# More pauses in two recurrences' instruction streams, UV's copies first, and an output projection by token halves with accumulators that end apart

## The chip, the core and the metric

The kernel runs on one core of one Trainium2 chip. The core has a matrix engine (TensorE, PE in the profile), a vector engine (VectorE, DVE), a scalar engine (ScalarE, ACT), GpSimd (POOL) and a sync engine (SP) that issues most transfers. The metric is the device time of one execution in microseconds, less being better. Three runs of the kernel before took 2685.09, 2686.59 and 2689.0 us, with a median of 2686.59 us.

## The reference

A decoder layer over 2048 tokens of width 1024, in float32. One input projection feeds two groups of heads, HGRN2 (a gated linear recurrence) and RWKV-7 (a recurrence with a vector-valued state update). Their outputs are concatenated, projected by `w_out` and added to `x`; a ConvFFN follows, and a last normalization.

```python
h = _rmsnorm(x, norm1_w[l])
proj = h @ w_in[l]
...
o_hg = _hgrn2_mixer(q_raw, f_raw, i_raw, g_raw, lower_bounds[l], hg_norm_w[l])
...
o_rw = _rwkv7_mixer(r, k, v, wd, ad, gd, ...)
x = x + jnp.concatenate([o_hg, o_rw], axis=-1) @ w_out[l]
x = x + _conv_ffn(_rmsnorm(x, norm2_w[l]), w_up[l], conv_w[l], conv_b[l], w_down[l])
```

## The kernel before

Tokens go through in four blocks of 512 (`nb` from 0 to 3). Phase 1 makes the input projection, both recurrences and the output projections of blocks 0 to 2; phase 2 makes the output projection of block 3 and the ConvFFN. The change touches phase 1 alone.

**Products in three passes.** A float32 product is computed as three matmuls of operands split in a high and a low part (`mm3`, lines 265, 266 and 267): high with high, high with low, low with high. I call these three a triple. A split (line 249 and line 250, or lines 242 and 243 for `split_to`) is a rounding copy on ScalarE and a subtraction on VectorE.

**Three streams.** `phase1` has three Python generators that write out instructions: `dense` (projections, transposes, output blocks), `rw_stream` (eight calls of `rw_super`, two for each token block) and `hg_stream` (16 calls of `hg_unit`, four for each token block). The loop at lines 1077 to 1084 goes in rounds: one step of `rw_stream`, one step of `hg_stream`, and then `fill(TICK)`, which takes steps of `dense` until 2000 ns of credit are used. A triple of a projection counts 648, one of an output block 680, whatever it takes on the chip. A step of a recurrence ends at a `yield`; with a `yield None` a stream says that its input isn't ready. So a `yield` more at one place lets one more portion of dense work stand between two steps of that recurrence. `dense` itself waits on counts of finished recurrence steps (`done`).

The Tile framework derives all dependencies, hands out buffers from a free pool for each tag (`bufs=4` means four buffers), and may issue ready instructions ahead of earlier ones that are not. The functions of ScalarE that need a table (`act`, line 112) keep the program's order among themselves.

**RWKV.** A step of `rw_super` makes a part of one chunked update for two head pairs. At line 702 `KB` is completed; at line 757 the inputs of the next super are released; lines 798 to 809 make `z` and copy it to `ZT`; lines 811 to 823 make `z2`. Lines 825 to 829 are the matmuls whose results are copied first to `M` (three copies, lines 831 to 834) and then to `UV` (four copies, lines 835 to 839). After the following `yield`, lines 844 to 850 multiply `KBT` with `UV`, and lines 851 to 863 use `M`. Lines 879 to 888 go through the eight chunks with the state `XH`.

**HGRN.** In `hg_unit`, lines 1003 to 1005 scale `k` and `q`; after a `yield`, lines 1010 to 1016 transpose `k` and make `KT`; after another, lines 1020 to 1026 use `KT` for the states.

**Output block.** `out_block` (line 373) goes through four passes, token halves `i2` by column halves `dh`. A pass has two accumulators (`accs`, tag `pj`, two PSUM banks that the projections use too), one for each 128 tokens, and eight slices `k` of the contracted dimension. For each slice the weights are loaded by POOL's queue (`woraw`, line 389) and split into `wh` and `wl` (tag `w`, four buffers each, which the projections' weights use as well); two triples follow, one for each accumulator. For blocks 0 and 1 the first pass also loads the recurrences' output `oT` slice by slice for all 512 tokens (line 382, staging tag `sg` with two buffers) and splits it into `hh` and `hl`. For block 2 the first 256 tokens were split before (`oh`, `ol`), and the others are loaded slice by slice in the third pass (line 386). At slice 6 two tiles of `x` are loaded (`xh`); at the end of the pass both accumulators are added to them (line 407) and stored (line 409). In the last pass `next_block` splits the next token block's input into `hh` and `hl`, two slices behind.

Of the kernel before, what the change touches and what calls it, by code (L numbers as in the profile page):

```python
# [7 lines left out]
F32 = mybir.dt.float32  # L8
# [10 lines left out]
P = 128  # L19
# [45 lines left out]
def tile_layer(ctx, tc, consts, x, norm1_w, w_in, hg_lb_logits, hg_norm_w, rw_shift_mu, rw_w0, rw_w2,  # L65
# [46 lines left out]
    def act(out_, in_, func, **kw):  # L112

        want = tables.get(func)
        if want is not None and want != tab["now"]:
            pre = S.preload_act_table_set(want)
# [3 lines left out]
        i_ = S.activation(out_, in_, func, **kw)  # L120
# [120 lines left out]
    def split_to(hi, lo, src):  # L241
        S.copy(hi, src)
        V.tensor_sub(lo, src, hi.bitcast(F32))

    def split(pool, src, shape, name, bufs):

        hi = pool.tile(shape, F32R, tag=name + "h", name=name + "h", bufs=bufs)
        lo = pool.tile(shape, F32R, tag=name + "l", name=name + "l", bufs=bufs)
        S.copy(hi, src)  # L249
        V.tensor_sub(lo, src, hi.bitcast(F32))  # L250
        return hi, lo
# [11 lines left out]
    def mm3(acc, lhs, rhs, first, last, skip=False):  # L263
        (lh, ll), (rh, rl) = lhs, rhs
        TE.matmul(acc, lh, rh, start=first, stop=False, skip_group_check=skip)  # L265
        TE.matmul(acc, lh, rl, start=False, stop=False, skip_group_check=skip)  # L266
        TE.matmul(acc, ll, rh, start=False, stop=last, skip_group_check=skip)  # L267

    def phase1(c1):
# [21 lines left out]
        def bank(kind):  # L291
            return ps.tile([P, 512], F32, tag=kind, name=kind, bufs=2)
# [7 lines left out]
        def stg(tag, name, bufs):  # L300
            return sp.tile([P, BLK], F32, tag=tag, name=name, bufs=bufs)
# [71 lines left out]
        def out_block(nb, oh=None, ol=None, then=None):  # L373


            for i2 in range(2):
                for dh in range(2):
                    accs = [bank("pj") for _ in range(2)]
                    for k in range(KD):
                        if i2 == 0 and dh == 0 and oh is None:  # L380
                            raw = stg("sg", "oraw", 2)
                            dma(raw, oT[nb][k * P:(k + 1) * P, :])
                            split_to(hh[:, k, :], hl[:, k, :], raw)
                        if i2 == 1 and dh == 0 and oh is not None:
                            raw = stg("sg", "oraw", 2)[:, 0:256]
                            dma(raw, oT[nb][k * P:(k + 1) * P, 256:512])
                            split_to(hh[:, k, 256:512], hl[:, k, 256:512], raw)
                        raw = wp.tile([P, 512], F32, tag="wraw", name="woraw", bufs=4)
                        wload(raw, w_out[0, k * P:(k + 1) * P, dh * 512:dh * 512 + 512])
                        wh, wl = split(wp, raw, [P, 512], "w", 4)  # L390
                        if k == KD - 2:
                            inputs = dh == 0 and (i2 == 0) == (oh is None)
                            xh = [wp.tile([P, BLK], F32, tag="wraw", name="xh", bufs=4) if inputs else
                                  stg("sg", "xh", 2) for _ in range(2)]
                            for q in range(2):
                                t0 = nb * BLK + (i2 * 2 + q) * P
                                dma(xh[q], x[0, t0:t0 + P, dh * 512:dh * 512 + 512])
                        for q in range(2):
                            is_ = slice((i2 * 2 + q) * P, (i2 * 2 + q + 1) * P)
                            lhs = ((hh[:, k, is_], hl[:, k, is_]) if oh is None or i2 == 1 else  # L400
                                   (oh[k // 4][:, k % 4, is_], ol[k // 4][:, k % 4, is_]))
                            mm3(accs[q], lhs, (wh, wl), k == 0, k == KD - 1)
                            if i2 == 1 and dh == 1 and q == 1:
                                next_block(then, k)
                            yield 680
                    for q in range(2):
                        V.tensor_add(xh[q], accs[q], xh[q])
                        r0 = (i2 * 2 + q) * P
                        dma(x1d[nb][r0:r0 + P, dh * 512:dh * 512 + 512], xh[q])

        rows = {}

# [225 lines left out]
        def rw_super(nb, s_):  # L638

            tl = stage[("tl", nb)]  # L640
            r, k, v = (stage.pop(("rkv", nb, s_, w)) for w in range(3))
            prs = (2 * s_, 2 * s_ + 1)
            pc = [slice(p * P, (p + 1) * P) for p in prs]

# [3 lines left out]
            def bank2():  # L648
                return ps.tile([P, 2, BLK], F32, tag="rw", name="rw", bufs=2)
# [52 lines left out]
            V.tensor_mul(KB[:, :, 1:3, :], v16(c), v16(a))  # L702
            V.tensor_mul(BV, b1, v)
            yield

            M = tile_("M", [2, 2, 4, 2, P], "M")
            for j in range(2):
# [48 lines left out]
            act(RHS[0:64, :, :, 0:64], tpv[64:128], AF.Copy)  # L756
            done["rw1"] += 1
            yield

            lv = bank2()  # L760
            for b, h, e, u in quads():
# [42 lines left out]
            for u in U:  # L804
                for e in range(2):
# [2 lines left out]
                    act(ZT[r1:r1 + 32, 8 * u:8 * u + 8],  # L808
                        z[c0:c0 + 32, 0, u * 256:u * 256 + 256].rearrange("p (s t) -> p s t", t=32), AF.Copy)
            yield  # L810
            z2 = bank2()
            for b, h, e, u in quads():
                r0 = er0(e)
# [17 lines left out]
            act(M[:, 0, 0, :, :, 0:64], quv[0][:, :, :, 0:64], AF.Copy)  # L831
            for e in range(2):
                r0, c0 = er0(e), col0(1, e)
                act(M[r0:r0 + 64, 0, 1, :, :, 0:64], quv[1][c0:c0 + 64, :, :, 0:64], AF.Copy)
            for u in U:
                for e in range(2):
                    r0, c0 = er0(e), col0(u, e)
                    act(UV[r0:r0 + 64, 4 * u:4 * u + 4, e, :].rearrange("p b (h t) -> p b h t", t=64),
                        quv[u][c0:c0 + 64, :, :, 64:128], AF.Copy)
            yield  # L840
            XH = tile_("XH", [2, 9, 64], "XH")
            V.tensor_copy(XH[:, :, 0, :], Xc[:, 2 * s_:2 * s_ + 2, :])
            xp = bank2()
# [79 lines left out]
        def hg_unit(nb, j):  # L923
# [79 lines left out]
            X = scaled(6)  # L1003
            V.tensor_mul(k, k, Sf)
# [12 lines left out]
            yield  # L1017
# [557 lines left out]
```

## Time and profile before

| | us |
|---|---|
| median of three runs | 2686.59 |
| the profiled execution's own time | 2686.26 |
| its span, from the first to the last instruction | 2684.5 |
| matmuls on PE, busy | 2614.7 |
| VectorE busy | 1929.6 |
| ScalarE busy | 1338.3 |
| PE busy in the first 100 us | 83.6 |
| PE busy from 1100 to 1200 us | 94.4 |
| PE busy from 1300 to 1400 us | 91.3 |

How to read it: a row of instructions has the engine, the line of the kernel, the operation, the tiles as out<-in, and the shapes. PEld are the weight loads, which run beside the matmuls. In a timeline the first two numbers are start and duration in us, and a bracket at the end gives the idle time before the row and what ended it. A row of waits reads "who line <- what it waited for: us in total, times, longest". A window's row gives its length, the busy time of PE, PEld, DVE, ACT and POOL with the number of instructions, the granted clock of PE as a share, the DMA engines' busy share and GB/s. Matmuls are pipelined: the duration shown (0.39 us for 128x512) includes the time in the pipe, and start to start they follow each other faster.

### The profile page before, as it was taken

What the parts mean: (1) busy time and instruction counts of PE and PEld (TensorE: products, weight loads), DVE (VectorE), ACT (ScalarE), POOL (GpSimd) and SP (SyncE); (2) the same over time, 40 slices, a digit from 0 to 9 for tenths busy, and PEclk for the clock granted to TensorE, in tenths of its full rate; (3) what the DMA queues carried; (4) which work ended last, traced back from release to release, by engine and by line L of the source; (5) the groups of instructions that cost most, each with busy time, mean ns of one, the idle gap of its engine ahead of it and who ended that gap; (6) DMA issues with size and microseconds to landing.
All of it is one profiled execution on the core that took longest, in us unless ns stands there. A gap on an engine that the chain in (4) does not pass through costs nothing.

```text
span 2684.5 us, 47831 instructions
## 1 busy us (share of the span) xinstructions
PE 2614.7 (97%) x18059; PEld 2091.1 (78%) x18059; DVE 1929.6 (72%) x3705; ACT 1338.3 (50%) x2158; POOL 381.8 (14%) x684
## 2 busy tenths in 40 slices
PE   7999999999999999999999999999999999999998
PEld 5777777777777777778778888887888888788887
DVE  4867757576466764657578789988998888676556
ACT  4555442454544545433357665456555545445444
POOL 6433222212222123222100000000000000000000
PEclk9999999999999999999899999999999999999999
DMA  8654543355643556834584458756764463898665
GB/s 304 198 166 162 166 135 117 115 161 195 197 149 116 157 161 214 290 115 132 160 272 149 134 184 267 243 171 194 259 200 149 149 202 124 311 325 282 203 192 184
DMA packets 312828, 510.52 MB, mean 190 GB/s; under 512 B 46879, under 2 KB 143509, under 8 KB 312597
## 3 DMA queue, kind: packets, MB, share of 16 engines
q1 hardware_dynamic: 258225, 329.65, 37.2%
q0 software_dynamic: 54304, 177.80, 20.3%
q8 instruction: 142, 2.33, 0.4%
q14 instruction: 89, 0.73, 0.1%
q10 hardware_dynamic: 68, 0.02, 0.0%
HBM read 373.13 MB, written 134.22 MB: 189 GB/s over the span
## 4 chain that ended last, share of the span: by engine, by line
PE 74%; DVE 7%; DMA 6%; issue 6%; ACT 5%; POOL 1%; SPq 0%; DVEq 0%; POOLq 0%; ACTq 0%
PE pj L265 8%; PE pj L266 7%; PE pj L267 7%; PE ua L265 5%; PE ua L267 5%; PE ua L266 5%; PE da L266 3%; PE da L267 3%; PE da L265 3%; PE ud L266 2%; PE ud L265 2%; PE ud L267 2%; PE hg L969 2%; PE db L265 2%; PE db L266 2%
## 5 line engine op out<-in xcount | busy, mean ns | idle before, releaser
L265 PE MATMUL pj<-hh,wh 128*128 128x512 f32 x960 | 404.1, 421 | 4.5 <-ACT rkv L120 1.7
L266 PE MATMUL pj<-hl,wh 128*128 128x512 f32 x960 | 377.9, 394 | 0.0
L267 PE MATMUL pj<-hh,wl 128*128 128x512 f32 x960 | 377.7, 394 | 0.0
L265 PE MATMUL ua<-Bh,uwh 128*128 128x512 f32 x704 | 275.9, 392 | 1.0 <-ACT m L120 0.9
L267 PE MATMUL ua<-Bh,uwl 128*128 128x512 f32 x704 | 274.3, 390 | 0.0
L266 PE MATMUL ua<-Bl,uwh 128*128 128x512 f32 x704 | 274.1, 389 | 0.0
L265 PEld LDWEIGHTS pj<-hh,wh 128*128 128x128 f32 x960 | 181.2, 189 | 59.6 <-issue 14.0
L267 PEld LDWEIGHTS pj<-hh,wl 128*128 128x128 f32 x960 | 181.0, 189 | 40.1 <-issue 0.6
L266 PEld LDWEIGHTS pj<-hl,wh 128*128 128x128 f32 x960 | 181.5, 189 | 38.7 <-issue 5.9
L249 ACT CAST uwh<-uraw 128x512 fp32r<-128x512 f32 x220 | 135.1, 618 | 138.0 <-PE ua L266 63.2
L250 DVE TENSOR_TENSOR dal<-draw,dah 128x512 fp32r<-128x512 f32 x138 | 95.3, 690 | 113.1 <-ACT dah L249 113.0
L250 DVE TENSOR_TENSOR uwl<-uraw,uwh 128x512 fp32r<-128x512 f32 x220 | 147.3, 686 | 34.8 <-ACT uwh L249 34.8
L249 ACT CAST dah<-draw 128x512 fp32r<-128x512 f32 x138 | 85.8, 622 | 167.3 <-PE da L266 78.7
L265 PEld LDWEIGHTS ua<-Bh,uwh 128*128 128x128 f32 x704 | 132.2, 188 | 29.8 <-ACT m L120 2.4
L267 PEld LDWEIGHTS ua<-Bh,uwl 128*128 128x128 f32 x704 | 132.2, 188 | 28.1 <-DVE uwl L250 0.4
L266 PEld LDWEIGHTS ua<-Bl,uwh 128*128 128x128 f32 x704 | 132.2, 188 | 26.6
L265 PE MATMUL ud<-Bh,uwh 128*128 128x512 f32 x352 | 138.0, 392 | 0.0
L267 PE MATMUL ud<-Bh,uwl 128*128 128x512 f32 x352 | 137.0, 389 | 0.0
L266 PE MATMUL ud<-Bl,uwh 128*128 128x512 f32 x352 | 137.0, 389 | 0.0
L1445 POOL DMA_DIRECT2D gd<-y x2 | 1.1, 556 | 947.0 <-DVE y L1443 947.0
L266 PE MATMUL da<-dbl,dah 128*128 128x512 f32 x332 | 129.5, 390 | 1.1 <-DVE dbl L250 1.1
L267 PE MATMUL da<-dbh,dal 128*128 128x512 f32 x332 | 129.2, 389 | 0.0
(570 smaller groups left out, 6199.2 us busy)
## 6 DMA issues: line engine op xcount, KB each, us to landing
uraw<-in_w_up_dram SPq DMA_DIRECT2D x176, 256.0 KB, 3.3
woraw<-in_w_out_dram POOLq DMA_DIRECT2D x96, 256.0 KB, 3.4
br<-gd SPq DMA_DIRECT2D x88, 256.0 KB, 4.1
draw<-Sg SPq DMA_DIRECT2D x88, 256.0 KB, 3.0
draw<-Tw SPq DMA_DIRECT2D x88, 256.0 KB, 3.5
gd<-y SPq DMA_DIRECT2D x86, 256.0 KB, 2.8
Sg<-br SPq DMA_DIRECT2D x72, 256.0 KB, 2.6
xt<-x1d SPq DMA_DIRECT2D x32, 512.0 KB, 5.9
```

Source lines behind the costliest of these rows:

```text
L249: S.copy(hi, src)
L250: V.tensor_sub(lo, src, hi.bitcast(F32))
L265: TE.matmul(acc, lh, rh, start=first, stop=False, skip_group_check=skip)
L266: TE.matmul(acc, lh, rl, start=False, stop=False, skip_group_check=skip)
L267: TE.matmul(acc, ll, rh, start=False, stop=last, skip_group_check=skip)
L969: TE.matmul(o, kt[:, t0:t0 + 64], qs, start=True, stop=True, tile_position=(0, e * 64))
L1445: (dma if end is None else nc.gpsimd.dma_start)(gd_[2 * h + b][fb * P:(fb + 1) * P, :], ys[0][:, b * BLK:(b + 1) * BLK])
```

## The change

Four things. `rw_super` takes an additional `yield` at four places (after lines 704, 758, 810 and 840) for the first six of its eight calls. `hg_unit` takes one more at two places (after lines 1006 and 1017) for the first 14 of its 16 calls. The four copies to `UV` come ahead of the three copies to `M`. And `out_block` is rewritten in two ways: `oT` is loaded and split by token halves, two slices at a time, the first half in pass one and the second in pass two (for block 2 only the second half); and the second accumulator runs one slice behind the first, so that the first one ends two triples earlier, and each is added and stored as soon as it ends. The tiles for `x` come from the weights' staging tag in the first pass of blocks 0 and 1 only, else from `sg`.

```diff
                     accs = [bank("pj") for _ in range(2)]
+                    ws, first_pass = [], oh is None and i2 == 0 and dh == 0
+                    pairs = {0: (0, 1), 2: (2,), 4: (3,)} if first_pass else {m: (m,) for m in range(4)}
                     for k in range(KD):
-                        if i2 == 0 and dh == 0 and oh is None:
-                            raw = stg("sg", "oraw", 2)
-                            dma(raw, oT[nb][k * P:(k + 1) * P, :])
-                            split_to(hh[:, k, :], hl[:, k, :], raw)
-                        if i2 == 1 and dh == 0 and oh is not None:
-                            raw = stg("sg", "oraw", 2)[:, 0:256]
-                            dma(raw, oT[nb][k * P:(k + 1) * P, 256:512])
-                            split_to(hh[:, k, 256:512], hl[:, k, 256:512], raw)
+                        if i2 == 0 and (dh == 1 or oh is None):
+                            hs = slice(256 * dh, 256 * dh + 256)
+                            for m in pairs.get(k, ()):
+                                raw = stg("sg", "oraw", 2).rearrange("p (k t) -> p k t", k=2)
+                                dma(raw, oT[nb][2 * m * P:(2 * m + 2) * P, hs].rearrange("(k p) t -> p k t", p=P))
+                                split_to(hh[:, 2 * m:2 * m + 2, hs], hl[:, 2 * m:2 * m + 2, hs], raw)
...
-                        wh, wl = split(wp, raw, [P, 512], "w", 4)
+                        ws.append(split(wp, raw, [P, 512], "w", 4))
...
-                        for q in range(2):
+                        for q, kq in ((0, k), (1, k - 1), (1, k if k == KD - 1 else -1)):
+                            if kq < 0:
+                                continue
...
-                            mm3(accs[q], lhs, (wh, wl), k == 0, k == KD - 1)
-                            if i2 == 1 and dh == 1 and q == 1:
+                            mm3(accs[q], lhs, ws[kq], kq == 0, kq == KD - 1)
+                            if kq == KD - 1:
+                                V.tensor_add(xh[q], accs[q], xh[q])
+                                r0 = (i2 * 2 + q) * P
+                                dma(x1d[nb][r0:r0 + P, dh * 512:dh * 512 + 512], xh[q])
+                            if i2 == 1 and dh == 1 and q == 1 and (kq == k or k < KD - 1):
                                 next_block(then, k)
                             yield 680
-                    for q in range(2):
-                        V.tensor_add(xh[q], accs[q], xh[q])
-                        r0 = (i2 * 2 + q) * P
-                        dma(x1d[nb][r0:r0 + P, dh * 512:dh * 512 + 512], xh[q])
...
+            more = range(1 if 2 * nb + s_ < 6 else 0)
...
             yield
+            for _ in more:
+                yield
...
+            for u in U:
+                for e in range(2):
+                    r0, c0 = er0(e), col0(u, e)
+                    act(UV[r0:r0 + 64, 4 * u:4 * u + 4, e, :].rearrange("p b (h t) -> p b h t", t=64),
+                        quv[u][c0:c0 + 64, :, :, 64:128], AF.Copy)
             act(M[:, 0, 0, :, :, 0:64], quv[0][:, :, :, 0:64], AF.Copy)
...
-            yield
+            for _ in range(2 if 4 * nb + j < 14 else 1):
+                yield
```

More of the change, by code (lines that the diff above doesn't have):

```diff
@@ L378, in out_block @@
                     accs = [bank("pj") for _ in range(2)]
+                    ws, first_pass = [], oh is None and i2 == 0 and dh == 0
+                    pairs = {0: (0, 1), 2: (2,), 4: (3,)} if first_pass else {m: (m,) for m in range(4)}
                     for k in range(KD):
-                        if i2 == 0 and dh == 0 and oh is None:
-                            raw = stg("sg", "oraw", 2)
-                            dma(raw, oT[nb][k * P:(k + 1) * P, :])
-                            split_to(hh[:, k, :], hl[:, k, :], raw)
-                        if i2 == 1 and dh == 0 and oh is not None:
-                            raw = stg("sg", "oraw", 2)[:, 0:256]
-                            dma(raw, oT[nb][k * P:(k + 1) * P, 256:512])
-                            split_to(hh[:, k, 256:512], hl[:, k, 256:512], raw)
+                        if i2 == 0 and (dh == 1 or oh is None):
[4 more added lines that the diff above has]
+                                split_to(hh[:, 2 * m:2 * m + 2, hs], hl[:, 2 * m:2 * m + 2, hs], raw)
                         raw = wp.tile([P, 512], F32, tag="wraw", name="woraw", bufs=4)
                         wload(raw, w_out[0, k * P:(k + 1) * P, dh * 512:dh * 512 + 512])
-                        wh, wl = split(wp, raw, [P, 512], "w", 4)
+                        ws.append(split(wp, raw, [P, 512], "w", 4))
                         if k == KD - 2:
-                            inputs = dh == 0 and (i2 == 0) == (oh is None)
-                            xh = [wp.tile([P, BLK], F32, tag="wraw", name="xh", bufs=4) if inputs else
+                            xh = [wp.tile([P, BLK], F32, tag="wraw", name="xh", bufs=4) if first_pass else
                                   stg("sg", "xh", 2) for _ in range(2)]
@@ L758, in rw_super @@
             yield
+            for _ in more:
+                yield
             lv = bank2()
@@ L810, in rw_super @@
             yield
+            for _ in more:
+                yield
             z2 = bank2()
@@ L830, in rw_super @@
             quv = [qus[u].rearrange("p j (b h t) -> p (j b) h t", h=2, t=P) for u in U]
[L831 to L834, printed above, removed]
             for u in U:
@@ L839, in rw_super @@
                         quv[u][c0:c0 + 64, :, :, 64:128], AF.Copy)
+            act(M[:, 0, 0, :, :, 0:64], quv[0][:, :, :, 0:64], AF.Copy)
+            for e in range(2):
+                r0, c0 = er0(e), col0(1, e)
+                act(M[r0:r0 + 64, 0, 1, :, :, 0:64], quv[1][c0:c0 + 64, :, :, 0:64], AF.Copy)
             yield
+            for _ in more:
+                yield
             XH = tile_("XH", [2, 9, 64], "XH")
@@ L1016, in hg_unit @@
             act(Af[0:64, :, 64:128], lp[0:64, 0:256].rearrange("p (b t) -> p b t", t=64), AF.Copy)
-            yield
+            for _ in range(2 if 4 * nb + j < 14 else 1):
+                yield
             SH = rp.tile([P, 5, P], F32, tag="SH", name="SH")
```

5 lines of the change are left out of this document (3 added, 2 removed).

## The prediction

> **What bounds the kernel now.** I read the page's busy times first.
>
> ```profile
> span 2684.5 us, 47831 instructions
> ...
> PE 2614.7 (97%) x18059; PEld 2091.1 (78%) x18059; DVE 1929.6 (72%) x3705; ACT 1338.3 (50%) x2158; POOL 381.8 (14%) x684
> ...
> PE 74%; DVE 7%; DMA 6%; issue 6%; ACT 5%; POOL 1%; SPq 0%; DVEq 0%; POOLq 0%; ACTq 0%
> ```
>
> TensorE is the bound, and the change removes none of its matmuls. It can gain only from PE's idle time, 2684.5 - 2614.7 = 69.8 us, and from time in which PE runs slowly. Everything touched lies in phase 1, whose last output block ends near 1350 us. So next the waits of PE in the window from 0 to 1350 us (total, times, longest):
>
> ```profile
> PE rw L848 <- ACT UV L120: 6.5, 6, 2.0
> PE pj L265 <- ACT hh L242: 6.4, 5, 2.2
> ...
> PE pj L265 <- DVE xh L407: 2.6, 4, 1.0
> PE hg L1011 <- DVE hk L1004: 2.4, 1, 2.4
> ...
> PE rw L815 <- ACT ZT L120: 1.5, 3, 0.8
> PE rw L885 <- DVE XH L887: 1.4, 3, 0.6
> ...
> PE pj L266 <- DVE wl L250: 0.9, 3, 0.4
> PE hg L1022 <- ACT KT L120: 0.8, 2, 0.4
> ...
> PE rw L714 <- DVE KB L702: 0.7, 2, 0.5
> PE pj L265 <- ACT wh L249: 0.7, 2, 0.4
> ```
>
> All but the XH row stand at places that the diff edits. None is long: this is a change of 20 us at most in 2686.
>
> The profiled execution took 2686.26 us, of which 2684.5 are the span; the median of the three runs is 2686.59. The sum below starts from 2686.26, and the 0.3 us between them are nothing here.
>
> **Pauses: do they cost rounds?** Each round of phase 1 runs one step of the RWKV stream, one of the HGRN stream, then 2000 ns of credit of dense work, where a triple of matmuls (L265 to L267) costs 648 or 680. I stepped the three generators through their yields and conditions (a count, no time): dense work never finds its condition unmet and sets 386 rounds, with the pauses as without. The streams wait 63 and 143 rounds for their inputs now, and would wait 39 and 115: 24 pauses (6 supers of 4) and 28 (14 units of 2) fit into these waits. A pause is therefore free as long as dense work is what lasts. If that were wrong, each of 24 would cost a round, 3.1 triples.
>
> A triple is three issue intervals of 0.23 us; the timeline of PE around the HGRN stall shows one at full clock, then the stall, then slow intervals:
>
> ```profile
> 1109.45 0.39 PE L266 MATMUL pj<-hl,wh 128*128 128x512 f32 x1
> 1109.67 0.39 PE L267 MATMUL pj<-hh,wl 128*128 128x512 f32 x1
> 1112.46 0.71 PE L1011 MATMUL hg<-ident,hk 128*128 128x128 f32 x4 [2.40 <-DVE hk L1004]
> ...
> 1115.17 0.63 PE L267 MATMUL pj<-hh,wl 128*128 128x512 f32 x1
> 1115.60 0.63 PE L265 MATMUL pj<-hh,wh 128*128 128x512 f32 x1
> ```
>
> So a triple is 0.69 us, and a pause puts 3.1 x 0.69 = 2.1 us of dense work in front of the next step. For UV the copies' order counts too:
>
> ```profile
> 151.21 1.80 ACT L120 ACTIVATE M<-rw 128x512 f32<-128x512 f32 x3
> ...
> 153.03 2.43 ACT L120 ACTIVATE UV<-rw 64x512 f32<-64x512 f32 x4
> ...
> 154.27 2.27 PE L848 MATMUL rw<-UV,KBT 128*64 128x64 f32 x64 [2.02 <-ACT UV L120]
> ```
>
> The three M copies (1.80 us) stand ahead of the UV copies that L848 waits for. With UV first these 1.80 us leave the wait in all eight supers; M is next needed by L862, behind the 2.2 us of L848, which cover it. Copy order and pause together clear all **6.5**. The pauses ahead of KT, behind KB and behind z take 0.8, 0.7 and 1.1 (the last super is not paused, so not all of ZT's 1.5); the 2.4 of L1011 lose 2.1. Sum: **11.2 us**.
>
> **Output projection.** Windows of the first and the third output block:
>
> ```profile
> 569.00:655.00 86.00, 81.76 (x941) 59.27 (x940) 65.92 (x146) 46.11 (x79) 15.20 (x29) 1.00 0.52 159
> ...
> 1295.00:1350.00 55.00, 49.93 (x448) 38.15 (x446) 33.47 (x74) 22.64 (x40) 8.11 (x15) 0.94 0.48 155
> ```
>
> In the third block (PE idle 5.1 of 55 us) the second token half is loaded in the pass that uses it, through two staging buffers:
>
> ```profile
> L386 SPq DMA_DIRECT2D oraw<-oT x8: 319/319/332, 1308.3 to 1324.8; - x8
> ...
> DMA to landing us min/median/max: 2.5/3.2/9.5
> ```
>
> and PE's waits from 1290 to 1350 us give the price:
>
> ```profile
> PE pj L265 <- ACT hh L242: 3.6, 2, 2.2
> ```
>
> Eight loads take 16.5 us to issue and 3.2 to land, while the 16 triples of a pass are 11.0 us. The change makes four loads of two slices out of them and puts them one pass earlier, on SP ahead of that pass's two x loads and two stores. I take 3.0 of 3.6, because the x tiles of two passes now share the same two staging buffers. The other 2.8 us of hh belong to the first two blocks, where a first pass splits weights and activations for each slice: two DVE splits of 0.69 against two triples of 1.38. By token halves it is one and a half; I take 1.9. The xh row (2.6) is a pass's first matmul waiting for the add that frees its bank. With the accumulators ending 1.38 us apart each add (0.68, as a split) has that cover in place of 0.69: I take 2.3. The wl and wh rows stay. Sum: **7.2 us**. Moved stores and adds are as many as before; an add waits in DVE's queue for its accumulator, with the next splits behind it.
>
> **Clock.** The 0.43 us intervals above are a halved clock. Three windows (the second-last number but two is the granted clock):
>
> ```profile
> 437.00:441.00 4.00, 4.00 (x36) 2.87 (x38) 3.07 (x6) 3.03 (x7) 1.68 (x2) 0.57 0.54 172
> 1112.00:1117.00 5.00, 4.54 (x20) 3.69 (x21) 3.60 (x9) 1.57 (x3) 1.07 (x2) 0.66 0.44 168
> ...
> 1310.00:1318.00 8.00, 6.28 (x32) 4.93 (x33) 4.09 (x11) 1.74 (x4) 0.00 (x0) 0.57 0.73 240
> ```
>
> Each loses (1 - clock) x length: 1.7, 1.7 and 3.4 us. The first follows stalls of ZT, the second the hk stall, the third the hh stall among unpaused XH stalls. I take both first ones and half of the third: **5.1 us**; bounds 0 and 6.8.
>
> The Trainium skill, "TensorE: Matmul & The Clock Gate", section "Why this matters for your kernels", states that throughput falls after an idle gap of about 3 us. Here the clock fell after an idle stretch of 2.40 us at most, so the trace is stricter than the page.
>
> **What the change costs.** (a) *Weights held longer.* The accumulators' lag keeps a slice's split weights until the second triple of the next slice. There are four buffers, but in blocks one and two the next projection's weights lie in two of them: loaded before the block, with the following ones only after it:
>
> ```profile
> 558.60 0.54 POOL L566 DMA_DIRECT2D wh<-Win281h  x1 [1.65 <-PE pj L267]
> ```
>
> ```profile
> 654.65 0.54 POOL L566 DMA_DIRECT2D wh<-Win160h  x1
> ```
>
> That two are left is seen in the split, which starts just when the matmuls two slices back end:
>
> ```profile
> 600.66 0.39 PE L267 MATMUL pj<-wh,hl 128*128 128x512 f32 x1
> ...
> 601.13 0.62 ACT L249 CAST wh<-woraw 128x512 fp32r<-128x512 f32 x1 [4.07 <-PE pj L267]
> ...
> 601.79 0.69 DVE L250 TENSOR_TENSOR wl<-woraw,wh 128x512 fp32r<-128x512 f32 x1 [0.96 <-ACT wh L249]
> ```
>
> ```profile
> ACT wh L249 <- PE pj L267: 21.6, 11, 4.1
> ```
>
> From the end of issue (600.66 + 0.23) to the end of wl (602.48) are 1.59 us; the first matmul needs only wh, so 1.59 - 0.23 = 1.36 must be covered. Now the next slice's two triples cover it: 1.38, just enough. In the new text nothing stands between: 1.36 us per slice, over 56 slices (7 of 8, 4 passes, 2 blocks) 76 us if PE kept that order and had no other work. If the order built from dependencies lets the lagging triple go first, 0.69 is covered, and the two freed buffers serve two slices: 0.33 per slice, 18 us. And of 86 us in a block only 64 x 0.69 = 44 are dense triples; the rest is mostly recurrence work that fills. I take a third of 18: **6 us**; bounds 0 and 76/3 = 25.
>
> (b) *Table loads.* ScalarE changes its function table in the program's order of Sigmoid/Tanh and Exp/Ln:
>
> ```profile
> L116 ACT ACT_TABLE_LOAD x44 | 56.5, 1283 | 1.5 <-PEq L1560 0.7
> ```
>
> The same counting of steps gives 42 changes now (44 in the row) and 56 with the pauses: 14 more at 1.283 us, 18 us on an engine that is half idle. I take a fifth: **4 us**; bounds 0 and 18. The Trainium skill, "ScalarE: Activation LUTs", section "What ACT_TABLE_LOAD costs", gives the same 1283 ns and adds a drain of about 1380 ns; by that the upper bound would be 37 us. No row here shows the drain.
>
> (c) *Switches.* Between dense and recurrence matmuls PE loses time:
>
> ```profile
> 1103.85 0.39 PE L267 MATMUL pj<-hh,wl 128*128 128x512 f32 x1
> 1104.16 1.59 PE L969 MATMUL hg<-hX 128*64 128x32 f32 x48
> 1105.69 0.50 PE L265 MATMUL pj<-hh,wh 128*128 128x512 f32 x1
> 1106.02 0.39 PE L266 MATMUL pj<-hl,wh 128*128 128x512 f32 x1
> ```
>
> 0.31 and 0.33 where an interval is 0.23, and by my estimate 0.1 at the block's own end: 0.3 per block. Rounds with recurrence matmuls rise from 250 to 256 by the count: **2 us**. (d) Steps that shift will stall elsewhere, as XH does now: **3 us**, bounds 0 and the 11.2 above.
>
> **Sum.** 11.2 + 7.2 + 5.1 = 23.5 gained, 6 + 4 + 2 + 3 = 15 given back: -8.5 us, 2686.26 - 8.5 = 2677.8.
>
> **Rivals.** *The weight buffers decide (slower).* In the first two blocks PE waits for wl at nearly every slice: 25 in place of 6 gives 2677.8 + 19 = 2696.8. It decides once more than about 14.5 us, 0.26 us of each of 56 slices, stay uncovered. For it: the split already starts on the release. Against: recurrence work is half of these windows, and more of it moves there. *Table loads on the path.* All 14 exposed: 2677.8 + 14 = 2691.8; against it, ACT is busy 50%. *Hidden anyway.* The recurrences' chains only move their waits, (d) = 11.2, gain from output and clock remaining: 2686. *The clock follows idle windows of over 3 us,* so no stall here moves it, and 5.1 falls away: 2682.9; the row against it is the 2.40 us stall. *No effect:* if Tile reorders PE's triples to the present order, the lag is gone and (a) with it: 2674, inside the forecast.
>
> **How the numbers follow.** Forecast 0.50 (its own range 2664 to 2682), buffers 0.20, tables 0.08, hidden anyway 0.12, clock 0.10. Least time: all gains without (a), (b), (d), 2686.26 - 25.2 + 2 = 2663. The range, 2663 to 2697, reaches from there to the price of the buffers' case; what lies beyond either end I hold below 2 in 10. About 0.2% (5.4 us) can be told from no change. Faster than 2681: nearly all of the forecast and some of clock and hidden, 0.54; within: the rest of these two, 0.16; slower than 2691.6: buffers, tables and a tail of hidden, 0.30.
>
> **What would show it.** Right: the L848, L1011 and third-block hh waits vanish, no halved clock near 437 and 1112 us, as many table loads as counted (56 to 58). Wrong: more waits on wl and wh between 569 and 655 us and a longer window for 64 triples, PE idle behind ACT rows where a table load stands, or dense work waiting for the streams.

## The result, and the profile after

The changed kernel takes 2700.02 us (median of 6 runs, 2692.16 to 2703.24) against 2685.84 us (6 runs, 2684.45 to 2689.0) for the kernel before: a ratio of 1.0051, 95% interval 1.0039 to 1.0063. It is 14 us slower; the forecast was 8.5 us faster, and the time lies above the range. The profiled execution took 2701.31 us. The head of its page:

```profile
span 2699.4 us, 47813 instructions
...
PE 2621.4 (97%) x18059; PEld 2089.2 (77%) x18059; DVE 1929.9 (71%) x3701; ACT 1356.9 (50%) x2168; POOL 380.9 (14%) x684
```

The same matmuls; PE is busy 6.7 us longer, and its idle time grows from 69.8 to 78.0 us. Windows split at the first matmul into phase 2's accumulators (1350.86 and 1363.36 us) show where. Before:

```profile
0.00:1350.86 1350.86, 1298.85 (x12257) 1007.54 (x12258) 873.65 (x2111) 628.90 (x1018) 367.76 (x658) 0.99 0.52 170
1350.86:2684.50 1333.64, 1315.83 (x5802) 1083.52 (x5802) 1055.94 (x1595) 709.41 (x1141) 14.07 (x26) 1.00 0.64 211
```

After:

```profile
0.00:1363.36 1363.36, 1304.27 (x12257) 1006.42 (x12258) 873.18 (x2105) 648.25 (x1029) 366.22 (x658) 0.99 0.51 168
1363.36:2699.40 1336.04, 1317.18 (x5803) 1082.81 (x5801) 1056.68 (x1596) 708.61 (x1140) 14.72 (x27) 1.00 0.64 211
```

Phase 1 is 12.5 us longer: 7.1 us of PE idle (length less busy, 52.0 to 59.1) and 5.4 us of busy time. The other 2.4 us lie in phase 2, whose text is unchanged. I use the same first window for every experiment below; "phase 1", "busy" and "idle" mean its numbers.

PE's waits from 0 to 1350 us after the change (line numbers have moved: 848 is now 858, 802 is 808, 1011 is 1022):

```profile
PE pj L265 <- ACT wh L249: 8.0, 8, 2.9
PE rw L808 <- DVE TZ L795: 5.2, 5, 2.1
PE pj L437 <- ACT xt L120: 4.2, 5, 2.0
PE rw L872 <- DVE AR L878: 3.0, 3, 1.0
...
PE rw L925 <- ACT yo L120: 2.9, 1, 2.9
PE rw L858 <- ACT M L120: 2.4, 3, 1.9
PE pj L266 <- DVE wl L250: 2.0, 3, 0.9
PE rw L885 <- DVE AR L878: 1.6, 1, 1.6
PE rw L823 <- ACT ZT L120: 1.5, 1, 1.5
PE rw L657 <- DVE yo L927: 1.3, 2, 0.9
...
PE hg L1022 <- DVE hk L1014: 1.1, 1, 1.1
...
PE pj L265 <- ACT hh L242: 0.9, 1, 0.9
...
PE hg L1034 <- ACT KT L120: 0.4, 1, 0.4
PE pj L265 <- DVE xh L405: 0.4, 2, 0.2
```

Read against the rows of before: what was aimed at went down. UV, hh, xh, hk, ZT, KT and KB were 20.9 us together; the rows in their places (UV's place is now M's) are 6.7. So 14.2 us were cleared, but the idle time rose by 7.1, so some 21.3 us are new. Five groups hold it: wh and wl 1.6 to 10.0, TZ 1.0 to 5.2, yo 0.6 to 4.2, xt at the transposes 1.7 to 4.2, AR 2.2 to 4.6, together 21.1; the other rows rose and fell by nearly the same amount. One row that fell did so in name only: the transposes of `k` (L1022, L1011 before) now also wait 1.3 us for `etmp` (L789) in the first output block, so that with the 1.1 for `hk` they wait 2.4 us as before.

The windows of before that had a halved clock, and the longest such stretch of after:

```profile
437.00:441.00 4.00, 4.00 (x21) 3.32 (x20) 3.79 (x13) 1.46 (x2) 1.07 (x2) 1.00 0.70 228
1112.00:1117.00 5.00, 5.00 (x73) 4.39 (x68) 4.86 (x18) 0.60 (x1) 1.14 (x3) 1.00 1.03 330
1295.00:1350.00 55.00, 52.15 (x800) 40.87 (x789) 38.50 (x87) 24.17 (x44) 10.27 (x19) 1.00 0.62 201
...
1144.60:1154.90 10.30, 8.77 (x122) 5.93 (x125) 5.91 (x13) 4.72 (x12) 2.16 (x4) 0.50 0.33 105
```

At the old places the clock is full. But a new stretch of 10 us follows a TZ stall, which the timeline of PE shows:

```profile
1141.07 0.39 PE L1044 MATMUL hg<-hq,SH 128*128 128x128 f32 x2
1143.02 0.75 PE L808 MATMUL rw<-TZ,M 32*32 32x32 f32 x64 [1.56 <-DVE TZ L795]
```

All halved stretches of phase 1 sum to 27.3 us in the trace after and 20.5 before: 3.4 us lost, where 5.1 were to be gained. That is most of the 5.4 us of busy time.

### The profile page after: what moved, and what is told of

Same layout as the page of the kernel before. It is cut to its first block, busy times and chain, and to the rows that moved or that the text cites. A ratio compares the mean times of both kernels' runs of the same rounds, so it can differ in the third digit from the quotient of the medians.

```text
span 2699.4 us, 47813 instructions
## 1 busy us (share of the span) xinstructions
PE 2621.4 (97%) x18059; PEld 2089.2 (77%) x18059; DVE 1929.9 (71%) x3701; ACT 1356.9 (50%) x2168; POOL 380.9 (14%) x684
## 4 chain that ended last, share of the span: by engine, by line
PE 51%; issue 5%; DVE 3%; DMA 3%; ACT 2%; POOL 1%; SPq 0%; POOLq 0%; DVEq 0%; ACTq 0%
PE ua L265 5%; PE ua L267 5%; PE ua L266 5%; PE da L266 3%; PE da L267 3%; PE da L265 3%; PE ud L267 3%; PE ud L266 3%; PE ud L265 3%; PE db L265 2%; PE db L266 2%; PE db L267 2%; PE pj L265 2%; PE pj L266 1%; PE pj L267 1%
## 5 line engine op out<-in xcount | busy, mean ns | idle before, releaser
L267 PE MATMUL pj<-hh,wl 128*128 128x512 f32 x960 | 377.9, 394 | 0.0
L267 PE MATMUL ua<-Bh,uwl 128*128 128x512 f32 x704 | 274.3, 390 | 0.0
L265 PEld LDWEIGHTS pj<-hh,wh 128*128 128x128 f32 x960 | 181.5, 189 | 55.2 <-issue 11.2
L267 PEld LDWEIGHTS pj<-hh,wl 128*128 128x128 f32 x960 | 181.3, 189 | 40.2 <-DMA wl<-Win251l 0.3
L267 PEld LDWEIGHTS ua<-Bh,uwl 128*128 128x128 f32 x704 | 132.2, 188 | 28.0 <-DVE uwl L250 0.4
L267 PE MATMUL ud<-Bh,uwl 128*128 128x512 f32 x352 | 137.0, 389 | 0.0
L267 PE MATMUL da<-dbh,dal 128*128 128x512 f32 x332 | 129.2, 389 | 0.0
```

## The experiments

All kernels compute the whole reference. Each ratio is against the kernel before, run beside it on the same chip (medians 2683.4 to 2685.5). It is formed from all executions and not from the two medians, so it can differ from their quotient by up to 0.1%; differences in us below are of medians where nothing else is said. In the expectations theory A is the weights' buffers held longer by the lag; the later ones say beside the letter what they claim.

| run | what differs from before | median us | ratio, 95% interval |
|---|---|---|---|
| e1_pauses | all 52 pauses | 2700.54 | 1.0052, 1.0037 to 1.0067 |
| e2_uv_first | UV's copies first | 2682.93 | 0.9996, 0.9982 to 1.0009 |
| e3_halves | output's inputs by token halves | 2682.94 | 0.9986, 0.9975 to 0.9998 |
| e4_lag | lagging second accumulator | 2696.7 | 1.0034, 1.0024 to 1.0044 |
| e5_late | next weights loaded after the block | 2690.07 | 1.0017, 1.0007 to 1.0028 |
| e6_lag_late | lag and that | 2684.62 | 0.9999, 0.9988 to 1.0011 |
| e7_rw_pauses | the 24 pauses of RWKV | 2702.48 | 1.0074, 1.0055 to 1.0093 |
| e8_hg_pauses | the 28 pauses of HGRN | 2683.52 | 0.9998, 0.9983 to 1.0013 |
| e9_tables | as many table loads as after | 2682.2 | 0.9990, 0.9979 to 1.0001 |
| e10_shift | two RWKV supers later, no pause | 2690.62 | 1.0025, 1.0014 to 1.0036 |
| e11_u0_first | copies of one tile pair first | 2680.32 | 0.9988, 0.9978 to 0.9998 |
| e12_parts | halves, lag in block 2, e11's order | 2672.89 | 0.9958, 0.9944 to 0.9971 |
| e13_rw_4_5 | RWKV pauses, supers 4 and 5 (8) | 2691.99 | 1.0028, 1.0016 to 1.0041 |
| e14_rw_0_3 | RWKV pauses, supers 0 to 3 (16) | 2693.98 | 1.0042, 1.0030 to 1.0054 |
| e15_rw_ahead | the two places ahead of `z` (12) | 2695.97 | 1.0050, 1.0037 to 1.0063 |
| e16_rw_behind | the two places behind `z` (12) | 2694.19 | 1.0036, 1.0023 to 1.0048 |
| e17_hgrn_odd | odd HGRN units later | 2681.72 | 0.9994, 0.9985 to 1.0004 |
| e18_hgrn_even | even HGRN units later | 2692.47 | 1.0038, 1.0025 to 1.0052 |

### The four parts, each alone

> The kernel before with the 24 + 28 pauses alone; copy order and output block as before. Theory A (the output block's lag is what costs, because two of the four weight buffers are taken): the pauses gain 3 to 8 us, 2678 to 2683. Theory B (the pauses cost, by 14 more table loads and by stalls moved to TZ, xt and the normalizations): 2690 to 2698. The page should show 58 table loads in place of 44 by either.

> The kernel before with UV's four copies ahead of M's three, nothing else. By the prediction's step the L848 wait on UV falls by most of its 6.5 us: 2681. By a rival read from the changed kernel's trace, L848 also needs the PSUM bank of the first half, which is free only after the two UV copies and the M copy of that half, the fifth copy in either order: no change, 2684 to 2688, and the wait is now put down to ACT M.

> The kernel before with oT's loads and splits by token halves alone; both accumulators end together as before. By the prediction 3.0 + 1.9 us of hh waits go: 2681. If the half clock near 1310 goes too: 2678. If the third block has no gain, 2686.

> The kernel before with the second accumulator one slice behind the first and each added as it ends; loads of oT as before. Theory A: 2692 to 2702, with more waits on wh and wl in the first two output blocks. Theory B: 2682 to 2688.

Each is the kernel before with that part of the diff and nothing else; e3 keeps the old order of triples and adds, e4 the old loads:

```diff
# e4_lag
-                        for q in range(2):
+                        for q, kq in ((0, k), (1, k - 1), (1, k if k == KD - 1 else -1)):
+                            if kq < 0:
+                                continue
```

The pauses cost 15 us, a little more than either theory expected, and the lag 11 (9 by the ratio); the halves gain a little, and the copies' order does nothing that can be told from no change. The parts add to 1.0068 where the whole has 1.0051, which is what the pauses alone have (1.0052).

The second sign that was expected of the lag, more waits on wh and wl, didn't come: they are 1.5 us in e4 (1.6 before). It is the pauses that raise them. In e1, without the lag, the rows that grew in the changed kernel are there already (before: hh 6.4, TZ 1.0, xt 1.7, wl 0.9, wh 0.7):

```profile
PE pj L265 <- ACT hh L242: 8.7, 9, 2.0
PE rw L807 <- DVE TZ L794: 5.5, 6, 2.1
PE pj L436 <- ACT xt L120: 4.2, 5, 2.0
PE pj L266 <- DVE wl L250: 3.2, 5, 1.0
PE pj L265 <- ACT wh L249: 3.0, 3, 2.3
```

**The copies.** In e2 the wait of the `KBT` matmuls didn't shrink, it changed its name:

```profile
PE rw L848 <- ACT M L120: 7.4, 7, 2.2
```

The timeline of the changed kernel shows it in super 7, which has no pauses:

```profile
1304.05 2.41 ACT L120 ACTIVATE UV<-rw 64x512 f32<-64x512 f32 x4
...
1306.48 1.82 ACT L120 ACTIVATE M<-rw 128x512 f32<-128x512 f32 x3
...
1307.13 2.09 PE L858 MATMUL rw<-UV,KBT 128*64 128x64 f32 x64 [1.85 <-ACT M L120]
```

L858 starts during the M copies, 0.65 us in, about when the first of the three is done (1.82 us for all three). It doesn't read M: its result `xp` takes a `rw` tile, and there are two, both held by `qus`. The first is free when all that reads `qus[0]` is done: two copies to UV and the first to M. In the order of before as in that of the change, that is the fifth copy of seven.

> The kernel before with the three copies of the first half (two of UV, one of M) ahead of the four of the second. If L848 waits for the PSUM bank of the first half, it starts after the third copy in place of the fifth: 1.2 us earlier, 3 to 6 us of its 6.5 go, 2680 to 2683, and the L848 row falls under 3. If it waits for all of UV, as the prediction had it: no change.

```diff
# e11_u0_first
+            for u in U:
+                for e in range(2):
...
+                if u == 0:
+                    act(M[:, 0, 0, :, :, 0:64], quv[0][:, :, :, 0:64], AF.Copy)
```

All copies of `qus[0]` first, those of `qus[1]` after. The row falls to less than half, and the kernel is the faster by 0.12%:

```profile
PE rw L849 <- ACT M L120: 3.0, 5, 0.9
```

It was expected below 3 and came to 3.0. So the explanation by the tile holds.

### The lag and the weights' buffers

> The kernel before, but the projection ahead of an output block doesn't load the next projection's weights, so that blocks one and two have all four weight buffers, as the third has. Control for the next run. The split no longer starts on the release of two slices back; the first projection after the block waits up to 3 us for its weights, twice. 2680 to 2690.

> The lag of the second accumulator, with all four weight buffers free in all output blocks. Theory A (two of four buffers taken make the lag costly): the lag alone cost 9 us; with the buffers it costs nothing or gains, so this run is 0 to 4 us below e5_late, and blocks one and two take 84 to 87 us as before, not 91 and 92. Rival (the lag itself, by more switches of PE between triples and recurrence matmuls, costs whatever the buffers): 7 to 10 us above e5_late, with some 40 switches in each block.

```diff
# e5_late, and with e4's lag e6_lag_late
-                load(i + 1)
+                if jobs[n + 1][0] != "O":
+                    load(i + 1)
```

The next projection's weights are no longer loaded ahead of an output block, so all four buffers serve the block. Alone that costs 4.9 us (2685.16 to 2690.07). With it, the lag gains 5.5 us (2690.07 to 2684.62); without it, the lag costs 11 (2685.45 to 2696.7). So the two occupied buffers are what makes the lag costly.

How much of this is the clock can be estimated, because the granted clock of every execution is on record: a mean clock of 1 - c costs about c times the span, 2.7 us for 0.001 (fitted over 29 executions of the kernel before, 0.001 less clock goes with 2.1 to 2.4 us more). The means are 0.9924 in e5 and 0.9948 in e6, a difference of 6.5 us, so the lag's gain in e6 is no more than a better clock, as e5's own loss is a worse one. Apart from the clock, in means, the lag costs about 2 us with free buffers (e5 to e6) and about 12 us without (before to e4, where the clock is slightly better than before). Windows from the first to the last triple of blocks 0 and 1, before:

```profile
569.70:655.40 85.70, 81.46 (x937) 59.02 (x936) 65.62 (x144) 45.47 (x77) 15.11 (x28) 1.00 0.51 158
917.00:1001.20 84.20, 80.57 (x936) 59.12 (x935) 63.25 (x134) 45.69 (x77) 15.01 (x28) 1.00 0.51 161
```

With the lag (e4):

```profile
570.50:661.80 91.30, 87.33 (x936) 60.76 (x936) 65.85 (x144) 45.61 (x77) 15.09 (x28) 0.98 0.47 149
922.80:1015.30 92.50, 90.14 (x936) 61.53 (x935) 63.96 (x135) 45.46 (x77) 15.08 (x28) 0.96 0.46 146
```

With the lag and free buffers (e6):

```profile
567.50:651.60 84.10, 79.22 (x938) 59.91 (x938) 64.34 (x145) 44.35 (x75) 15.12 (x29) 0.98 0.48 158
915.00:1000.10 85.10, 82.71 (x937) 61.27 (x936) 62.15 (x137) 44.37 (x75) 15.68 (x30) 0.94 0.48 156
```

The same 936 instructions take 5.6 and 8.3 us more in e4, and none of it is idle (4.2 to 4.0 us and 3.6 to 2.4): PE is busy longer. ScalarE waits longer to split the next weights (for block 0, in e4; the row of before is 21.6, 11, 4.1):

```profile
ACT wh L249 <- PE pj L267: 28.7, 13, 4.4
```

Where a triple must wait for its weights, recurrence matmuls fill the gap, in smaller pieces: the trace has 40 and 38 changes from dense to recurrence matmuls in the two windows of e4, 26 and 27 before, 23 and 27 in e6. The clock column explains 1.8 and 3.7 us of it. What is left, 3.8 and 4.6 us over 14 and 11 more changes, is 0.27 and 0.42 us for each, near step (c)'s 0.3.

In the changed kernel this cost doesn't show. Its blocks 0 and 1 take 87.2 and 85.1 us (from 557.5 and from 925.7 us) with 708 and 862 matmuls, because the pauses move recurrence work out of them; with the pauses alone (e1) they take 86.3 and 85.2 us with 753 and 865.

### Which pauses, and what of them

> Only the 24 pauses of the RWKV stream. By the count of table changes 8 more loads than before (52 in phase 1). If table loads are what the pauses cost: 2691 to 2697, more than half of the 15 us. If the place of the HGRN steps costs: 2684 to 2688.

> Only the 28 pauses of the HGRN stream. By the count no table load more (44 in phase 1). If table loads are what the pauses cost: 2682 to 2687. If the place of the HGRN steps costs: 2690 to 2697.

> The kernel before with an activation of one element that needs a third table, ahead of the second pause's place in the first seven supers: up to 14 more table loads, no pause. If table loads are what the pauses cost: 2693 to 2703. If they hide behind the half idle ScalarE: 2685 to 2690.

> The kernel before with 12 rounds' delay ahead of the fourth super and 4 ahead of the sixth, and no pause inside a super: their forward substitutions (62 VectorE operations each) fall into rounds 164 to 172 and 258 to 266, as with the pauses, that is into the output blocks that begin at rounds 159 and 262; 2 table loads more by the count. Theory C (the pauses cost because they push this chain into the passes that VectorE's splits bound): 2692 to 2700. If it is the pauses' number or the table loads: 2684 to 2689.

```diff
# e9_tables: one element, in the first seven supers
             done["rw1"] += 1
             yield
+            if 2 * nb + s_ < 7:
+                act(dum[:, 0:1], dum[:, 1:2], AF.Silu)
...
# e10_shift: rw_stream, ahead of supers 3 and 5
+                for _ in range({3: 12, 5: 4}.get(n, 0)):
+                    yield
```

(In e9 the added activation stands before that `yield`.) The cost is all of RWKV's pauses: e8 is even with before, and e7 is as slow as e1, slower than either of its expectations. Table loads from 0 to 1350 us, after and in e9, in this order:

```profile
L116 ACT ACT_TABLE_LOAD x57 | 73.1, 1283 | 1.7 <-PEq L1572 0.7
```

```profile
L116 ACT ACT_TABLE_LOAD x58 | 74.4, 1283 | 1.7 <-PEq L1564 0.7
```

e9 has as many as the changed kernel and costs nothing, and e13 below, with no load more than before, costs 0.28%: table loads are out. e10 takes no pause inside a super; it starts two supers later, so that their triangular substitution runs inside output blocks 0 and 1, as it does with the pauses. That costs 6 us (2685.06 to 2690.62), between its two expectations. So moving these steps has a price without any pause, about a third of e7's 17 us (2685.16 to 2702.48). Phase 1 of e7, and its waits:

```profile
0.00:1364.94 1364.94, 1301.18 (x12257) 1008.28 (x12258) 871.83 (x2109) 639.23 (x1026) 367.67 (x657) 0.99 0.51 168
```

```profile
PE pj L265 <- ACT hh L242: 7.9, 10, 1.6
PE hg L1020 <- DVE hk L1013: 4.8, 3, 2.4
PE pj L265 <- ACT wh L249: 4.5, 3, 2.4
PE rw L807 <- DVE TZ L794: 3.8, 4, 2.9
...
PE rw L656 <- DVE yo L926: 2.7, 4, 0.9
...
PE rw L857 <- ACT UV L120: 2.0, 3, 1.0
```

The pauses do for this wait on UV what they should, 6.5 to 2.0 us, though another one (L768, L763 before) grew from 0.2 to 1.7. But idle rises from 52.0 to 63.8 us, which is 11.8 of the 14.1 us by which phase 1 is longer: hk, wh, TZ and yo, at 2.4, 0.7, 1.0 and 0.6 before, take 11.1 us more.

### Is it one place, or one super?

> All four pauses, in the fifth and sixth super alone: the sixth super's substitution falls into rounds 259 to 267, in the second output block; no table load more. Read from e7's starts of supers, the stretch from the fifth super to the seventh lost 10.7 us: 2694 to 2699. If only the shift costs, about half of e10's: 2687 to 2690. If the cost goes by the number of pauses, 8 of 24: 2690 to 2693.

> All four pauses, in the first four supers alone: the fourth super's substitution in rounds 166 to 174, in the first output block; 8 table loads more. By e7's starts of supers: 5 to 7 us, 2690 to 2693. If the cost goes by the number of pauses, 16 of 24: 2696 to 2699.

> Only the two pauses ahead of the substitution, in six supers: rounds 160 to 168 and 257 to 265 for the chains, so that both lie in the output blocks. If place in the output blocks decides: 2692 to 2700. If the pauses behind the substitution are what costs: 2685 to 2689.

> Only the two pauses behind the substitution, in six supers: rounds 158 to 166 and 255 to 263, so that the fourth super's chain lies in the first output block and the sixth's mostly ahead of the second. If place decides: 2688 to 2692, the loss in the first block alone. If the pauses behind the substitution are what costs: 2693 to 2700.

Edits: the condition in `more` becomes `2 * nb + s_ in (4, 5)` or `2 * nb + s_ < 4` (e13, e14), or only two of the four places have the pause (e15, e16). Every part costs something: 0.28% and 0.42% for the supers, 0.50% and 0.36% for the places, 0.74% for all. In the profiled phase 1 the idle time goes the same way as the length (from 1350.86, 52.0): e13 1358.47, 56.9; e14 1363.34, 62.8; e15 1360.22, 59.6; e16 1351.16, 55.0; e10 1355.98, 57.7. The profiled execution of e16 took less than its median, so it says little. No place and no super carries the cost: e15 came where the place in the output blocks was to decide, e16 where the pauses behind the substitution were to, and each answer excludes the other. The parts add up to about the whole (0.28 + 0.42 and 0.50 + 0.36, against 0.74 with an interval from 0.55 to 0.93), which makes 0.7 to 1.1 us for each RWKV pause. So a price for each of these pauses is not excluded; e14 lies below what the number of pauses gave (2696 to 2699), and the 28 pauses of HGRN show no such price.

### Rounds with recurrence work, or any delay

From these runs I had a fit: 1.2 us for each added round that holds recurrence matmuls. The last two runs were to test it, with RWKV untouched.

> The kernel before with five yields ahead of each odd HGRN unit (1 to 13), seven units in all; RWKV untouched. By the count of steps the rounds that carry recurrence matmuls rise from 250 to 268, table loads from 42 to 44, dense work never waits. Theory D (the time goes with the number of these rounds, some 1.2 us for each added round, as a fit over the kernels with pauses has it): +18 rounds are about +21 us, 2706, and more blocks of recurrence matmuls in the first 1350 us. Rival (the cost is bound to RWKV's own steps): within 4 us of before, 2685.

> The same five yields ahead of the even HGRN units (0 to 12), seven units in all. By the count the rounds with recurrence matmuls stay 250, table loads 44. Theory D: within 3 us of before, 2685. Rival (any delay of these streams costs by itself): as much as e17_hgrn_odd.

```diff
# e17_hgrn_odd; e18_hgrn_even has n % 2 == 0
                 while ready["hg"] <= n:
                     yield None
+                for _ in range(5 if n % 2 == 1 and n < 14 else 0):
+                    yield
```

The rounds are counted from the generators' steps. The fit (theory D) fails in both: 18 more of those rounds cost nothing, and a delay that adds none costs 9 us (2683.43 to 2692.47). The rival of e17, that the cost is bound to RWKV's own steps, holds there, but e18 shows that delays of HGRN can cost as much. In phase 1 the trace of e17 even has 321 stretches of recurrence matmuls against 298 before, so a switch as such isn't 0.3 us wherever it stands either. Phase 1 of e17, then of e18:

```profile
0.00:1346.99 1346.99, 1297.38 (x12257) 1007.20 (x12257) 873.07 (x2111) 632.81 (x1020) 368.76 (x658) 0.99 0.51 170
```

```profile
0.00:1356.51 1356.51, 1308.55 (x12258) 1016.07 (x12258) 885.93 (x2111) 634.58 (x1020) 366.65 (x658) 0.98 0.51 169
```

e18 is idle less than before (48.0 us) and busy 9.7 us more. Its clock was halved for 47.8 us of phase 1 in the trace, 27.3 more than before, which is 13.6 us of work. One window holds a third of it:

```profile
566.00:584.00 18.00, 16.30 (x144) 10.98 (x146) 12.44 (x25) 7.17 (x14) 0.54 (x1) 0.53 0.42 131
```

A stall precedes it in PE's timeline, just ahead of the first output block:

```profile
564.63 0.66 PE L969 MATMUL hg<-hX 128*64 128x32 f32 x16 [2.43 <-DVE hX L950]
```

This isn't one execution's chance. The mean clock of all five executions of e18 is 0.9898, of the kernel before 0.9945: 12.7 us by the estimate above, more than its whole loss (8.8 us in means). RWKV's pauses lose 7.9 of 19.3 us so (e7, 0.9915 against 0.9945), and e10 almost nothing (0.2 of 6.2). So a delay can cost as much by a halved clock as another does by many waits; that the stall at 564 us is what halves it is read from their order in time, not tested. e17 and e18 differ in nothing but which units are late.

### What can be kept

> What the runs so far speak for: oT by token halves in all blocks, the lag in the third block alone (where all four weight buffers are free), the first half's copies first, and no pause. By the stages: about 5 to 7 us from the third block and 3 from the copies: 2675 to 2680.

The halves in all blocks, the lag in block 2 alone, where all four buffers are free, e11's order, and no pauses:

```diff
# e12_parts
+                        for q, kq in (((0, k), (1, k)) if oh is None else
+                                      ((0, k), (1, k - 1), (1, k if k == KD - 1 else -1))):
```

2672.89 us, 0.42% under the kernel before, faster than both, and 2 us below what was expected. Its phase 1:

```profile
0.00:1340.35 1340.35, 1294.54 (x12257) 1005.00 (x12258) 870.42 (x2105) 627.36 (x1013) 366.21 (x658) 0.99 0.51 171
```

10.5 us shorter: 6.2 less idle, 4.3 less busy. The halves and the order alone have 0.14% and 0.12%. Block 2 is 84.0 us from first to last triple (90.8 before, 84.4 in e3), so the lag itself shows little there; that the rest is the lag was not tested by itself. By the clocks of all executions (0.9963 against 0.9944) about 5 us of the gain are a better clock.

## Why the prediction was wrong, point by point

- **"A pause is therefore free as long as dense work is what lasts."** This is the step that failed. The count behind it doesn't speak of time inside a round, where PE waits for a step that is late beside other work. All 52 pauses cost 15 us (e1), as much as the whole change, and the 24 of RWKV alone 17 us (e7), where the forecast had them gain 11.2 and give back 3 by shifted stalls, 4 by table loads and 2 by switches. e7's trace has 11.8 us more idle, and by the mean clocks some 8 us more are lost to a halved clock. The 28 HGRN pauses did cost nothing (e8). The count itself held: it gives the table loads of the runs (52 in e7, 44 in e8, 58 in e1). I had priced such stalls as step (d), 3 us with a bound of 11.2, what the old waits were worth; but a delayed step can hit other waits than the old ones, so the bound wasn't one. The rival "hidden anyway" named the mechanism and stopped at the same bound.
- **"Copy order and pause together clear all 6.5."** The copy order clears nothing (e2): I took the wait's releaser as the last operand and didn't ask what the output's tile waits for. The M row was reachable from the listing: two `rw` tiles, three users. With the pauses 4.1 of 6.5 went. The other pauses took 1.3 of 2.1 (hk, where `etmp` took its place), 0.4 of 0.8 (KT), all 0.7 (KB) and none of 1.1 (z): 6.5 of 11.2.
- **Output, 7.2.** Right as waits: hh lost 5.5 (forecast 4.9) and xh 2.2 (2.3). The halves alone removed the hh row and gained 0.14% (e3), 3.8 us; in the trace block 2 went from 90.8 to 84.4 us. The lag alone cut xh to 0.9 (e4).
- **Clock, 5.1.** The places named were cleared, as forecast; it was halved elsewhere, behind new stalls, a net loss of 3.4 in the trace. The term needed a counterpart: whatever moves a recurrence may make such a stall as well as remove one.
- **(a), 6 with bounds 0 and 25.** Right mechanism for the lag alone, and too small: it costs 9 to 11 us net (e4), and apart from the clock the taken buffers are some 10 us of it (about 12 without free buffers, 2 with them). It came as more switches, not as waits on wh. In the changed kernel the rival "the weight buffers decide" had its sign: wh waits 8.0 us, all in blocks 0 and 1. But wh and wl rise to 6.2 us by the pauses alone (e1) and not at all by the lag alone (e4), and the whole change costs no more than the pauses; so that the lag costs anything beside the pauses is not shown.
- **(b), 4.** The count was right (44 and 14 more; the window to 1350 us, which now ends inside phase 1, has 57, and one more follows before its end), the price is 0 (e9).
- **(c), 2.** What remains of the 5.4 us of busy time after the clock is 2.0, as forecast, but e17 shows that this isn't a price for each switch: the agreement is luck.
- **Tile reorders the triples, 2674.** It doesn't undo the lag: with the lag alone blocks 0 and 1 are 5.6 and 8.3 us longer, and the split of their weights waits longer for L267 (28.7 us for 21.6 in block 0).

**What stays open**: why RWKV's delays cost and those of HGRN may or may not. The new waits are spread over some ten rows and differ from kernel to kernel; the number of rounds with recurrence work, table loads, place and super are excluded as the one cause, the number of RWKV's pauses is not. Part of it, some 8 of 19 us in e7, is a halved clock, and what halves it is not tested either. That the added time is the luck of how steps of three streams meet on VectorE and ScalarE fits e17 and e18, but is only argued.

## What to carry to other kernels

A spare round isn't spare time: moving a step of a stream that shares engines with others re-deals all waits behind it, so price it from a run, or leave an upper bound far above the waits it removes. When a wait has a releaser that the instruction doesn't read, look at the output's buffer, and free it first. Before work is made to overlap further, count the buffers that are free at that place, not those declared; here the lag alone cost some 12 us with two of four taken and some 2 with all four free, the clock left aside. And compare the granted clocks of all executions before a difference of a few us is put down to a mechanism.

## What was not expected of the hardware

- Stalls of 1.56 us (after, 1143 us) and 2.43 us (e18, 564 us) ahead of small matmuls were followed by 10 and 17 us of halved clock, while one of 1.85 us (after, 1307 us) was followed by none (the window from 1295 to 1350 us has a clock of 1.00). The Trainium skill, "TensorE: Matmul & The Clock Gate", section "Why this matters for your kernels", has throughput drop mid-kernel after PE was idle for more than about 3 us. All three gaps are shorter, so here the measurements decide, and the length of the gap alone doesn't order them.
- 14 more table loads of 1.283 us, 18 us on ScalarE, didn't move the time (e9, 0.9979 to 1.0001).
- A shortage of buffers can show as busy PE time and not as waits: in e4 PE's idle time fell by 3.8 us (52.0 to 48.2) while phase 1 grew by 9.7, with as much halved clock in phase 1 as before (20.5 us in both traces).
